# A two-layer encoder trunk: the norms' transposed copies on two engines, and block-sum steps later in some pairs of weight columns

## The chip, the cores and the metric

The kernel runs on one core of a Trainium2 chip. The metric is the device time of one execution in microseconds (us). A core has a matrix engine (TensorE, PE in the profile), a vector engine (VectorE, DVE), an activation engine (ScalarE, ACT), a general one (GpSimd, POOL) and a queue engine that issues loads here (SyncE, SP). They run side by side and wait for one another through semaphores; each runs its own instructions in program order. TensorE adds its products up in PSUM, in banks of 128 partitions by 512 floats; the other operands lie in SBUF.

## The reference

256 tokens of width 2048 pass through two layers. The first mixes tokens by attention, the second by a gated recurrence; each is followed by a gated feed-forward block (FFN) with 5632 hidden features. All is float32.

```python
def swiglu(h, w_gate, w_up, w_down):
    return (jax.nn.silu(h @ w_gate) * (h @ w_up)) @ w_down

for i in range(DEPTH):
    h = rms_norm(x, norm_mix[i])
    mix = attention_mixer(h, ...) if i % 2 == 0 else recurrent_mixer(h, ...)
    x = x + mix
    x = x + swiglu(rms_norm(x, norm_ffn[i]), ffn_w_gate[i], ffn_w_up[i], ffn_w_down[i])
```

`rms_norm` divides each token's row by the root of its mean square and scales each feature.

## The kernel before, in words

**Products.** Each float32 number is split into a high part and the rest (`hi` and `lo`, for weights; two halves of one tile for the other operand), and a product is three matmuls: hi times hi, hi times lo, lo times hi. Weights come in halves of 512 KB: SyncE's queue loads one into `raw`, ScalarE casts it to `hi` (L120), VectorE subtracts to get `lo` (L121). There are five buffers of each of the three, so a load starts when VectorE has read the raw half of five loads earlier, and a cast when TensorE is done with the half of five loads earlier.

**Pairs.** The FFN takes two output column blocks of 512 at a time (`project_pair`): gate and up together, or two columns of the down product. A pair keeps four PSUM banks (`acc`; two blocks by two groups of 128 tokens). It goes through its inner dimension in steps of two tiles of 128 features, two weight halves to a step. A gate/up pair has 8 steps over the 16 norm tiles `xg`. The hidden features come in three parts of 12, 16 and 16 tiles: a down pair of the first part has 6 steps, the others 8. A plain step is 24 matmuls. A block-sum step (steps 2 and 5 of 8, 1 and 3 of 6; `SEVEN`) is the seven-product form of a 2 by 2 block product, 21 matmuls: `seven_forms` adds weight blocks on VectorE (L245 to L248, into `wx`, which has one buffer), ScalarE casts the three sums (`wxh`, L252), VectorE subtracts (`wxl`, L253). Three of its products go to four extra banks `pm`, and after the pair's last block-sum step `merge` combines those on ScalarE and VectorE (L311 to L315) while TensorE goes on with the steps that are left.

**Ends of pairs.** After its last step a pair's banks are added on VectorE: to the merged blocks in a gate/up unit (L755, L758, each block followed by the nonlinearity), to the residual `x_tok` in a down product (L498; the merged blocks are added to it at L489). The next pair starts in the same four banks, one after the other, 6 matmuls each, so it wants the bank adds in that order.

**Turning.** Tokens lie on partitions in `x_tok`; the operands of the products need features there. `turned` does it for 512 features: two 32x32-blockwise transposes on VectorE into `tb`, then 16 copies of 32 partitions by 256 on ScalarE (L445) that put the blocks in place in `tf`. `tb` and `tf` have one buffer each. It serves two callers. `Norm.add` turns each of the four columns of `x_tok` as it is finished, and scales it into four `xg` tiles (hi on ScalarE L396, lo on VectorE L397): 12 calls. The FFN unit turns its 512 hidden features and casts them into four `act` tiles (L764, L765): 22 calls. In the unit the four hidden tiles of part 0 that come last are tiles 8 to 11, which steps 4 and 5 of a six-step pair multiply. Where a norm or a unit has both tiles of a block-sum step, `x_forms` makes that step's sums of the other operand (`nf`, `hf`).

**Order.** TensorE's order is the order of the program text. `ffn_order` lists the weight halves in the order in which pairs take them, which is the order of SyncE's loads. ScalarE's and VectorE's order is set by a scheduler, which places instructions by its own estimate of when their inputs are there.

Of the kernel before, what the change touches and what calls it, by code (L numbers as in the profile page):

```python
# [21 lines left out]
KT = D // P  # L22
# [4 lines left out]
DFF = 5632  # L27
PARTS = [12, 16, 16]
SEVEN = {6: (1, 3), 8: (2, 5)}
HALF = 8  # L30
WIDE = 512
NCOL = D // WIDE
FOUR = WIDE // P
# [37 lines left out]
def trunk(ctx, tc, w, out):  # L71
    nc = tc.nc
    act, dve, pool, pe, sync = nc.scalar, nc.vector, nc.gpsimd, nc.tensor, nc.sync
# [13 lines left out]
    def nm(s):  # L87
        uid[0] += 1
        return f"{s}_{uid[0]}"
# [17 lines left out]
    def load_half(src, n, pieces=1, then=None, before=None):  # L107
        raw = wp.tile([P, HALF, P], F32, tag="raw", name=nm("raw"), bufs=5)
        hi = wp.tile([P, HALF, P], F32R, tag="hi", name=nm("hi"), bufs=5)
        lo = wp.tile([P, HALF, P], F32R, tag="lo", name=nm("lo"), bufs=5)  # L110
        newest["load"] = sync.dma_start(out=raw[:, :n, :], in_=src[:, :n, :])
        newest["raw"] = raw
        if then:
            then()
        if before:
            before(raw)
        for i in range(pieces):
            sl = slice(i * n // pieces, (i + 1) * n // pieces)
            newest["tiles"] = hi, lo
            newest["cast"] = act.copy(hi[:, sl, :], raw[:, sl, :])  # L120
            dve.tensor_tensor(lo[:, sl, :], raw[:, sl, :], hi[:, sl, :].bitcast(F32), ALU.subtract)  # L121
        return [(hi[:, i, :], lo[:, i, :]) for i in range(n)]


    def halves(src, kt):
        return [(src[:, a : min(a + HALF, kt), :], min(HALF, kt - a)) for a in range(0, kt, HALF)]

    def wide(name):
        src = w[name]
        return [(src[c, i], HALF) for c in range(src.shape[0]) for i in range(src.shape[1])]  # L130

    def ffn_order(l):
        units = [wide(f"w_gate{l}"), wide(f"w_up{l}")]
        seq, i = [], 0
        for p, n in enumerate(PARTS):
            for _ in range(n // FOUR):
                seq += sum(zip(*(u[i : i + KT // 2] for u in units)), ())
                i += KT // 2
            down = wide(f"w_down{l}_{p}")
            for c in range(0, len(down), n):  # L140
                seq += sum(zip(down[c : c + n // 2], down[c + n // 2 : c + n]), ())
        return seq

    order = [(w["w_k"][i], HALF) for i in range(len(KEY_TILES))]
    order += sum((halves(w["w_qv"][h % 20], KT) for h in range(NQ, NQ + 20)), [])
    order += wide("w_o") + ffn_order(0)
    for b in range(-1, NBLK):
        xin = range(2 * b + 2, 2 * b + 4) if b + 1 < NBLK else []
        yin = range(KT + 2 * b, KT + 2 * b + 2) if b >= 0 else []
        both = [halves(w["w_in"][c], KT) for c in (*xin, *yin)]  # L150
# [35 lines left out]
    def step():  # L186
        clock[0] += 1
        due = [i for i, (t, _) in enumerate(waiting) if t <= clock[0]]
        if due:
            waiting.pop(due[0])[1]()  # L190
# [5 lines left out]
    def new_acc():  # L196
        return ps_a.tile([P, 2 * S], F32, tag="acc", name=nm("acc"))
# [37 lines left out]
    def flat(t):  # L235
        return t.rearrange("p (k c) f -> p k (c f)", k=2)
# [29 lines left out]
        dve.tensor_tensor(t[:, 1], y[:, 4:, :], t[:, 0].bitcast(F32), ALU.subtract)  # L266
        return [(t[:, 0, i, :], t[:, 1, i, :]) for i in range(4)]

    def project_pair(xs, forms, middle):
        banks = [[new_acc() for _ in range(2)] for _ in range(2)]  # L270
        begun = set()

        def product(acc, x, wt, last=False):
            for i, (a, b) in enumerate(((x[0], wt[0]), (x[0], wt[1]), (x[1], wt[0]))):
                pe.matmul(acc, a, b, start=id(acc) not in begun, stop=last and i == 2)  # L275
                begun.add(id(acc))
            step()
            step()

        def tokens(k, a):  # L280
            return [xs[k][:, o + a * P : o + (a + 1) * P] for o in (0, S)]

        end = len(xs) // 2 - 1
        for n in range(end + 1):
            if n in forms:
                s1, s2, s3, s4 = forms[n]
                b11, b21, t3, b22, t1, t2, t4 = seven_forms()
                if n == min(forms):
                    p1, q6, q5, q7 = (ps_m.tile([P, WIDE], F32, tag="pm", name=nm("pm")) for _ in range(4))
                last = n == max(forms)  # L290
                product(p1, tokens(2 * n, 0), b11, last)
                product(banks[0][0], tokens(2 * n + 1, 0), b21)
                product(banks[1][0], s4, b22)
                product(q7, s3, t3, last)
                product(q5, s1, t1, last)
                product(q6, s2, t2, last)
                product(banks[0][1], tokens(2 * n + 1, 1), t4)
                if last:
                    middle(p1, q5, q6, q7)
            else:  # L300
                for j in range(2):
                    half()
                    hi, lo = (flat(t) for t in newest["tiles"])
                    for a in range(2):
                        for k in range(2):
                            product(banks[j][a], tokens(2 * n + k, a), (hi[:, k, :], lo[:, k, :]), n == end and k == 1)
        return banks

    def merge(p1, q5, q6, q7):
        g, u = (fp[0].tile([P, 2, WIDE], F32, tag=t, name=nm(t), bufs=1) for t in ("fg", "fu"))  # L310
        act.copy(g[:, 0, :], p1)  # L311
        dve.tensor_tensor(g[:, 1, :], q6, g[:, 0, :], ALU.subtract)
        dve.tensor_tensor(u[:, 0, :], q5, g[:, 1, :], ALU.add)
        dve.tensor_tensor(g[:, 1, :], q7, g[:, 1, :], ALU.subtract)
        dve.tensor_tensor(u[:, 1, :], u[:, 0, :], q7, ALU.subtract)  # L315
        return g, u
# [66 lines left out]
    class Norm:  # L383
# [18 lines left out]
        def add(self, c):  # L402
            for a in range(2):
                act.activation(tmp("nj", (P, WIDE), bufs=1), x_tok[:, a, c, :], AF.Square, accum_out=self.sums[:, a, c : c + 1])
            for f in turned(x_tok[:, :, c, :]):
                self.operand(f, True)
            for n in SEVEN[KT // 2] if self.seven else ():
                if FOUR * c <= 2 * n < FOUR * c + FOUR:
# [24 lines left out]

    def turned(src):
        b = fp[0].tile([P, 2, FOUR, P], F32, tag="tb", name=nm("tb"))
        f = fp[0].tile([P, 8, FOUR, 32], F32, tag="tf", name=nm("tf"))
        for a in range(2):
            dve.transpose(b[:, a, :, :], src[:, a, :])  # L440
        for q in range(4):
            for i in range(4):
                o, y = f[32 * i : 32 * i + 32, q::4, :, :], b[32 * q : 32 * q + 32, :, i, :]
                y = y.rearrange("p a (k t) -> p a k t", k=FOUR)
                act.copy(o, y)  # L445
        return [f[:, :, k, :] for k in range(FOUR)]

    fp = []
# [65 lines left out]
    def table_act(*a, **k):  # L514
        table_op(act.activation(*a, **k))

    def ln_exp_tables():
        table_op(act.preload_act_table_set("natural_log_exp_and_others"))
# [191 lines left out]
    def act_tile():  # L710
        return xp.tile([P, 2 * S], F32R, tag="act", name=nm("act"), bufs=18)
# [35 lines left out]


    def ffn(norm, nxt):
        def unit(hid, forms, seven):  # L750
            got = []
            banks = project_pair(norm.xs, norm.forms, lambda *banks: got.extend(merge(*banks)))
            g, u = got
            for a, acc in enumerate(banks[0]):
                dve.tensor_tensor(g[:, a, :], acc, g[:, a, :], ALU.add)  # L755
                table_act(g[:, a, :], g[:, a, :], AF.Silu, scale=norm.rt[:, a : a + 1])
            for a, acc in enumerate(banks[1]):
                dve.tensor_tensor(u[:, a, :], acc, u[:, a, :], ALU.add)  # L758
                dve.scalar_tensor_tensor(u[:, a, :], u[:, a, :], norm.rt[:, a : a + 1], g[:, a, :], ALU.mult, ALU.mult)
            first = len(hid)  # L760
            for f in turned(u):
                h = act_tile()
                hi, lo = (h[:, o : o + S].rearrange("p (q t) -> p q t", t=32) for o in (0, S))
                act.copy(hi, f)  # L764
                dve.tensor_tensor(lo, f, hi.bitcast(F32), ALU.subtract)  # L765
                hid.append(h)
            for i, n in enumerate(seven):
                if first <= 2 * n < len(hid):
                    forms[n] = x_forms(hid[2 * n], hid[2 * n + 1], f"hf{i}")

        for p, n in enumerate(PARTS):
            hid, forms = [], {}
            for _ in range(n // FOUR):
                unit(hid, forms, SEVEN[n // 2])
            last = p == len(PARTS) - 1
            if last and nxt is not None:
                ln_exp_tables()
            down(hid, forms, nxt if last else None, last and nxt is None)
# [106 lines left out]
    units = [(d, j) for j in range(2) for d in range(2)]  # L885
# [114 lines left out]
```

## Time and profile before

| what | us |
|---|---|
| three runs: lowest, median, highest | 2032.6, 2037.86, 2040.56 |
| the profiled execution | 2037.47 |
| its span | 2035.7 |
| TensorE busy in it | 1996.2 (98%) |
| VectorE busy | 1692.5 (83%) |
| ScalarE busy | 1369.3 (67%) |

The span is what the profiler saw between the first and the last instruction. Each row of a timeline is a start, a duration, the engine, the line, the operation, what it writes and reads (tile names without numbers), and in brackets the idle time before it with what ended it. The profile shows also the TensorE clock that the throttle granted, 1.00 being full speed; over the profiled span it was 0.992.

### The profile page before, as it was taken

How to read it: one execution, taken by the hardware profiler on the slowest of the kernel's cores; microseconds unless marked ns; L12 is line 12 of the kernel's file. 1: busy time of each engine (PE TensorE's matmuls, PEld its weight loads, DVE VectorE, ACT ScalarE, POOL GpSimd, SP SyncE). 2: the span in 40 equal slices, each digit the busy share in tenths (PEclk: the TensorE clock that was granted, in tenths of full speed). 3: DMA queues.
4: the chain of work that ended last, by engine and by line, in shares of the span. 5: the costliest groups of instructions: out<-in, count | busy, mean ns of one | idle time of the engine just before them, and what ended most of it. 6: DMA issues, size and time to landing. Idle time of an engine off the chain costs nothing.

```text
span 2035.7 us, 27908 instructions
## 1 busy us (share of the span) xinstructions
PE 1996.2 (98%) x9920; PEld 1689.5 (83%) x9920; DVE 1692.5 (83%) x2351; ACT 1369.3 (67%) x2166; POOL 168.7 (8%) x213
## 2 busy tenths in 40 slices
PE   9999999999999999999799999999999999999999
PEld 8898878878888888887699998878788878888887
DVE  8998678987888888888679887688897888878887
ACT  7665876664667446677789988767745766457663
POOL 1563000000000000000133330000000000000000
PEclk9999999999999999999899999999999999999999
DMA  8444555556555665655456554656556556655564
GB/s 320 156 135 145 194 180 194 188 191 196 191 201 183 222 197 189 205 184 196 155 172 187 184 176 158 207 167 205 186 188 195 188 199 213 196 193 187 199 217 145
DMA packets 109003, 386.06 MB, mean 190 GB/s; under 512 B 12224, under 2 KB 12992, under 8 KB 108736
## 3 DMA queue, kind: packets, MB, share of 16 engines
q1 hardware_dynamic: 108720, 384.26, 57.1%
q8 instruction: 78, 1.28, 0.2%
q14 instruction: 61, 0.50, 0.1%
q10 hardware_dynamic: 144, 0.02, 0.0%
HBM read 382.13 MB, written 2.10 MB: 189 GB/s over the span
## 4 chain that ended last, share of the span: by engine, by line
PE 47%; issue 42%; DVE 7%; DMA 2%; ACT 2%; POOL 0%; SPq 0%; DVEq 0%; ACTq 0%; POOLq 0%
PE acc L275 23%; PE acc L228 4%; PE acc L206 4%; PE pm L275 3%; DVE lo L121 3%; PE acc L319 3%; PE acc L320 3%; PE acc L321 3%; PE pm L320 1%; PE pm L321 1%; PE pm L319 1%; DMA raw<-in_w_up_dram 1%; ACT tf L445 1%; ACT hi L120 1%; DMA raw<-in_w_down_dram 0%
## 5 line engine op out<-in xcount | busy, mean ns | idle before, releaser
L120 ACT CAST hi<-raw 128x1024 fp32r<-128x1024 f32 (+1 forms) x708 | 727.6, 1045 | 477.6 <-PE acc L275 372.1
L121 DVE TENSOR_TENSOR lo<-raw,hi 128x1024 fp32r<-128x1024 f32 (+1 forms) x708 | 852.4, 1223 | 135.3 <-ACT hi L120 133.9
L275 PE MATMUL acc<-hi,xg 128*128 128x512 f32 x2200 | 697.7, 390 | 3.0 <-DVE fg L755 2.9
L275 PEld LDWEIGHTS acc<-hi,xg 128*128 128x128 f32 x2200 | 413.8, 188 | 95.5 <-issue 6.4
L275 PE MATMUL acc<-lo,xg 128*128 128x512 f32 x1100 | 428.6, 390 | 0.0
L275 PE MATMUL acc<-hi,act 128*128 128x512 f32 x1072 | 342.6, 391 | 0.9 <-DVE fg L755 0.7
L275 PEld LDWEIGHTS acc<-lo,xg 128*128 128x128 f32 x1100 | 207.0, 188 | 42.3
L275 PEld LDWEIGHTS acc<-hi,act 128*128 128x128 f32 x1072 | 201.9, 188 | 48.4 <-issue 3.0
L445 ACT COPY tf<-tb 32x256 f32<-32x256 f32 x544 | 219.5, 404 | 9.2 <-DVE xg L397 1.0
L275 PE MATMUL acc<-lo,act 128*128 128x512 f32 x536 | 209.2, 390 | 0.0
L228 PE MATMUL acc<-hi,act 128*128 128x512 f32 x512 | 159.9, 390 | 0.0
L319 PE MATMUL acc<-xg,hi 128*128 128x256 f32 x512 | 147.0, 287 | 11.7 <-ACT xg L396 11.7
L320 PE MATMUL acc<-xg,hi 128*128 128x256 f32 x512 | 146.6, 286 | 0.5 <-DVE xg L397 0.5
L245 DVE TENSOR_TENSOR wx<-raw,raw 128x512 f32<-128x512 f32 x68 | 47.0, 691 | 119.7 <-DMA raw<-in_w_up_dram 91.5
L321 PE MATMUL acc<-xg,lo 128*128 128x256 f32 x512 | 146.0, 285 | 0.0
L253 DVE TENSOR_TENSOR wxl<-wx,wxh 128x1536 fp32r<-128x1536 f32 x68 | 119.1, 1752 | 22.4 <-ACT wxh L252 22.1
L206 PE MATMUL acc<-xg,hi 128*128 128x512 f32 x384 | 125.7, 396 | 0.2 <-ACT hi L120 0.2
L252 ACT CAST wxh<-wx 128x1536 fp32r<-128x1536 f32 x68 | 100.3, 1476 | 34.5 <-DVE wx L248 34.5
L275 PEld LDWEIGHTS acc<-lo,act 128*128 128x128 f32 x536 | 100.9, 188 | 20.4
L228 PEld LDWEIGHTS acc<-hi,act 128*128 128x128 f32 x512 | 96.1, 188 | 19.6
L319 PEld LDWEIGHTS acc<-xg,hi 128*128 128x128 f32 x512 | 99.8, 195 | 12.1 <-ACT xg L396 12.1
L320 PEld LDWEIGHTS acc<-xg,hi 128*128 128x128 f32 x512 | 99.7, 195 | 1.1 <-DVE xg L397 1.0
(238 smaller groups left out, 2830.4 us busy)
## 6 DMA issues: line engine op xcount, KB each, us to landing
raw<-in_w_gate_dram SPq DMA_DIRECT2D x176, 512.0 KB, 4.4
raw<-in_w_up_dram SPq DMA_DIRECT2D x176, 512.0 KB, 4.3
raw<-in_w_down_dram SPq DMA_DIRECT2D x176, 512.0 KB, 4.3
raw<-in_w_in_dram SPq DMA_DIRECT2D x64, 512.0 KB, 4.5
raw<-in_w_qv_dram SPq DMA_DIRECT2D x40, 512.0 KB, 4.3
raw<-in_w_o_dram SPq DMA_DIRECT2D x32, 512.0 KB, 3.6
raw<-in_w_out_dram SPq DMA_DIRECT2D x32, 512.0 KB, 4.3
graw<-in_w_gates_dram SPq DMA_DIRECT2D x32, 256.0 KB, 3.5
```

The lines of the kernel that those rows point to most:

```text
L120: newest["cast"] = act.copy(hi[:, sl, :], raw[:, sl, :])
L121: dve.tensor_tensor(lo[:, sl, :], raw[:, sl, :], hi[:, sl, :].bitcast(F32), ALU.subtract)
L206: pe.matmul(o, w, x, start=(k == 0 and not part), stop=(k == total - 1 and not part))
L228: pe.matmul(accs[a], x, wt[:, k, :], start=(k0 + k == 0 and n == 0), stop=(end and k == 1 and n == 2))
L245: dve.tensor_tensor(x[:, 0, :], r2[:, 0, :], r1[:, 0, :], ALU.add)
L252: act.copy(xh, x)
L253: dve.tensor_tensor(xl, x, xh[:].bitcast(F32), ALU.subtract)
L275: pe.matmul(acc, a, b, start=id(acc) not in begun, stop=last and i == 2)
L319: pe.matmul(o, hi, x[:, :S], start=start, stop=False)
L320: pe.matmul(o, hi, x[:, S:], start=False, stop=False)
L321: pe.matmul(o, lo, x[:, :S], start=False, stop=stop)
L445: act.copy(o, y)
```

## The change

It has three parts. In `turned`, the odd two of every four copies go to VectorE when the norms call it: 96 of the 192 copies of the 12 calls. The units pass `False` and keep ScalarE for all 16. In the first gate/up pair of each layer the steps run in the order 0, 1, 3, 4, 2, 6, 5, 7, so that the block-sum steps 2 and 5 stand fifth and seventh. In each pair of six steps the order is 0, 2, 1, 4, 3, 5, so that block-sum steps 1 and 3 stand third and fifth; there are two such pairs in each layer. The loads follow (`ffn_order`), and the first and last block-sum step, and the last step, are taken from the new order. All other pairs keep theirs. The number of matmuls, loads and casts stays.

```diff
+USUAL_STEPS = {6: (0, 2, 1, 4, 3, 5), 8: (0, 1, 2, 3, 4, 5, 6, 7)}
+FIRST_STEPS = (0, 1, 3, 4, 2, 6, 5, 7)
...
+    def pair_steps(n, first=False):
+        return FIRST_STEPS if first else USUAL_STEPS[n]
+
     def ffn_order(l):
...
-                seq += sum(zip(*(u[i : i + KT // 2] for u in units)), ())
+                for k in pair_steps(KT // 2, i == 0):
+                    seq += [u[i + k] for u in units]
                 i += KT // 2
             down = wide(f"w_down{l}_{p}")
             for c in range(0, len(down), n):
-                seq += sum(zip(down[c : c + n // 2], down[c + n // 2 : c + n]), ())
+                for k in pair_steps(n // 2):
+                    seq += [down[c + k], down[c + n // 2 + k]]
...
-    def project_pair(xs, forms, middle):
+    def project_pair(xs, forms, middle, first=False):
...
-        end = len(xs) // 2 - 1
-        for n in range(end + 1):
+        steps = pair_steps(len(xs) // 2, first)
+        seven = [n for n in steps if n in forms]
+        for n in steps:
             if n in forms:
...
-                if n == min(forms):
+                if n == seven[0]:
...
-                last = n == max(forms)
+                last = n == seven[-1]
...
-                            product(banks[j][a], tokens(2 * n + k, a), (hi[:, k, :], lo[:, k, :]), n == end and k == 1)
+                            product(banks[j][a], tokens(2 * n + k, a), (hi[:, k, :], lo[:, k, :]), n == steps[-1] and k == 1)
...
-    def turned(src):
+    def turned(src, both=True):
...
-                act.copy(o, y)
+                if i % 2 and both:
+                    dve.tensor_copy(o, y)
+                else:
+                    act.copy(o, y)
...
-            for f in turned(u):
+            for f in turned(u, False):
...
-            for _ in range(n // FOUR):
-                unit(hid, forms, SEVEN[n // 2])
+            for i in range(n // FOUR):
+                unit(hid, forms, SEVEN[n // 2], p == i == 0)
```

Three places show what this does to the order of an engine's instructions. The numbers behind the names tell tiles apart; a line such as L498 of the kernel before is L509 in the changed one.

VectorE at the end of the first six-step pair of layer 0, before. `lo` are halves of the next pair's weights, `fg` and `fu` the merged blocks, `acc_4364`, `4366`, `4365` and `4367` the four banks, in the order in which the next pair wants them:

```order
L314 TENSOR_TENSOR fg_4528<-pm_4428,fg_4528 128x512
L315 TENSOR_TENSOR fu_4529<-fu_4529,pm_4428 128x512
L489 TENSOR_TENSOR x_tok<-x_tok,fu_4529 128x512
L246 TENSOR_TENSOR raw_4664<-raw_4664 128x512
L121 TENSOR_TENSOR lo_4657<-raw_4655,hi_4656 128x1024
L498 TENSOR_TENSOR x_tok<-x_tok,acc_4364 128x512
L489 TENSOR_TENSOR x_tok<-x_tok,fg_4528 128x512
L489 TENSOR_TENSOR x_tok<-x_tok,fu_4529 128x512
L247 TENSOR_TENSOR wx_4661<-raw_4664,raw_4655 128x512
L498 TENSOR_TENSOR x_tok<-x_tok,acc_4366 128x512
L121 TENSOR_TENSOR lo_4666<-raw_4664,hi_4665 128x1024
L498 TENSOR_TENSOR x_tok<-x_tok,acc_4365 128x512
```

The same place in the changed kernel:

```order
L252 TENSOR_TENSOR wx_4697<-raw_4700,raw_4691 128x512
L509 TENSOR_TENSOR x_tok<-x_tok,acc_4364 128x512
L321 TENSOR_TENSOR fu_4565<-pm_4463,fg_4564 128x512
L253 TENSOR_TENSOR raw_4700<-raw_4700 128x512
L322 TENSOR_TENSOR fg_4564<-pm_4464,fg_4564 128x512
L323 TENSOR_TENSOR fu_4565<-fu_4565,pm_4464 128x512
L500 TENSOR_TENSOR x_tok<-x_tok,fu_4565 128x512
L123 TENSOR_TENSOR lo_4675<-raw_4673,hi_4674 128x1024
L254 TENSOR_TENSOR wx_4697<-raw_4700,raw_4691 128x512
L500 TENSOR_TENSOR x_tok<-x_tok,fg_4564 128x512
L500 TENSOR_TENSOR x_tok<-x_tok,fu_4565 128x512
L509 TENSOR_TENSOR x_tok<-x_tok,acc_4366 128x512
```

The merge now stands between the first and the second bank add, and a sum of the next block-sum step's weights (`wx_4697`, which reads the load `raw_4700`) ahead of both. After the last row shown come `lo_4693`, `wx_4697`, and then the adds of `acc_4365` and `acc_4367`.

ScalarE in the first six-step pair of layer 0, before. `tf_4333` holds the hidden features of the unit just ended, `act_4352` and `act_4355` are hidden tiles 8 and 9, `wxh` the block-sum step's weight sums:

```order
L120 CAST hi_4496<-raw_4495 128x1024
L120 CAST hi_4540<-raw_4539 128x1024
L445 COPY tf_4333<-tb_4332 32x2x128 x16
L120 CAST hi_4558<-raw_4557 128x1024
L252 CAST wxh_4493<-wx_4492 128x1536
L120 CAST hi_4576<-raw_4575 128x1024
L764 CAST act_4352<-tf_4333 128x256
L764 CAST act_4355<-tf_4333 128x256
```

And in the changed kernel:

```order
L122 CAST hi_4505<-raw_4504 128x1024
L456 COPY tf_4333<-tb_4332 32x2x128 x16
L122 CAST hi_4523<-raw_4522 128x1024
L122 CAST hi_4532<-raw_4531 128x1024
L122 CAST hi_4576<-raw_4575 128x1024
L775 CAST act_4352<-tf_4333 128x256
L775 CAST act_4355<-tf_4333 128x256
L775 CAST act_4358<-tf_4333 128x256
L775 CAST act_4361<-tf_4333 128x256
L259 CAST wxh_4529<-wx_4528 128x1536
```

The cast of the sums has gone behind the casts of the hidden tiles. On TensorE the plain step 4, which multiplies tiles 8 and 9, stands ahead of the second block-sum step instead of behind it.

ScalarE at the last norm column of layer 0's FFN, before. `nj` is the norm's square sum, `tf_3237` the turned column, `xg` the norm tiles, `wxh_3362` the sums of the first pair's first block-sum step:

```order
L404 ACTIVATE nj_3234,nsq_2358<-x_tok 128x512
L120 CAST hi_3365<-raw_3364 128x1024
L120 CAST hi_3402<-raw_3401 128x1024
L445 COPY tf_3237<-tb_3236 32x2x128 x16
L515 ACTIVATE rsq_s_3272<-nrt_3268 128x2
L252 CAST wxh_3362<-wx_3361 128x1536
L120 CAST hi_3420<-raw_3419 128x1024
```

And in the changed kernel:

```order
L412 ACTIVATE nj_3234,nsq_2358<-x_tok 128x512
L456 COPY tf_3237<-tb_3236 32x2x128 x8
L122 CAST hi_3374<-raw_3373 128x1024
L404 ACTIVATE xg_3256<-tf_3237,pk 128x256
L404 ACTIVATE xg_3259<-tf_3237,pk 128x256
L404 ACTIVATE xg_3262<-tf_3237,pk 128x256
L404 ACTIVATE xg_3265<-tf_3237,pk 128x256
L122 CAST hi_3392<-raw_3391 128x1024
L526 ACTIVATE rsq_s_3272<-nrt_3268 128x2
L122 CAST hi_3410<-raw_3409 128x1024
L526 ACTIVATE nr_3271<-rsq_s_3272 128x2
L122 CAST hi_3428<-raw_3427 128x1024
```

Eight copies are left there, the norm tiles come directly behind them, and the cast of the sums (`wxh_3434`) has moved two rows past the end of what is shown.

More of the change, by code (lines that the diff above doesn't have):

```diff
@@ L749, in ffn, with unit @@
     def ffn(norm, nxt):
-        def unit(hid, forms, seven):
+        def unit(hid, forms, seven, first):
             got = []
-            banks = project_pair(norm.xs, norm.forms, lambda *banks: got.extend(merge(*banks)))
+            banks = project_pair(norm.xs, norm.forms, lambda *banks: got.extend(merge(*banks)), first)
             g, u = got
```

## Prediction

> **What bounds the kernel now.** I read the page first, for the engines' shares, then the waits of TensorE, and then the timeline around each wait that the change touches.
>
> ```profile
> span 2035.7 us, 27908 instructions
> PE 1996.2 (98%) x9920; PEld 1689.5 (83%) x9920; DVE 1692.5 (83%) x2351; ACT 1369.3 (67%) x2166; POOL 168.7 (8%) x213
> ```
>
> TensorE is busy for 98% of the span, so the time moves only by what it waits for, and by what its clock does after a wait. About 39 us separate its busy time from the span. Which engine it waited for (total, times, longest):
>
> ```profile
> PE acc L319 <- ACT xg L396: 11.7, 2, 8.4
> PE pm L275 <- ACT wxh L252: 6.3, 4, 2.0
> PE pm L275 <- DVE wxl L253: 6.2, 5, 1.3
> PE acc L275 <- DVE fg L755: 3.6, 6, 1.4
> ```
>
> The first row is the start of the recurrence; rows two and three are block-sum steps that want their three cast weight sums; the last is the start of a pair that wants its accumulator banks back. One such block-sum step, in the first gate/up pair:
>
> ```profile
> 274.38 6.65 ACT L445 COPY tf<-tb 32x256 f32<-32x256 f32 x16
> 281.16 1.46 ACT L252 CAST wxh<-wx 128x1536 fp32r<-128x1536 f32 x1
> ...
> 282.65 1.76 DVE L253 TENSOR_TENSOR wxl<-wx,wxh 128x1536 fp32r<-128x1536 f32 x1 [5.32 <-ACT wxh L252]
> ...
> 281.08 0.39 PE L275 MATMUL pm<-hi,nf 128*128 128x512 f32 x1
> 282.67 0.50 PE L275 MATMUL pm<-wxh,nf 128*128 128x512 f32 x1 [1.20 <-ACT wxh L252]
> 284.46 0.50 PE L275 MATMUL pm<-wxl,nf 128*128 128x512 f32 x1 [1.29 <-DVE wxl L253]
> ...
> 288.91 0.39 PE L275 MATMUL acc<-lo,xg 128*128 128x512 f32 x1
> ```
>
> The cast of the sums stands on ScalarE behind the norm's 16 copies; VectorE's wxl follows the cast; TensorE waits for both. How fast the matmuls then run (stretch, TensorE busy with its count, the other engines, granted clock, DMA):
>
> ```profile
> 283.00:288.20 5.20, 3.91 (x12) 2.93 (x12) 5.20 (x7) 5.10 (x9) 0.00 (x0) 0.73 0.27 83
> 290.00:300.00 10.00, 10.00 (x45) 8.28 (x45) 7.84 (x10) 5.39 (x5) 0.00 (x0) 1.00 0.72 241
> ```
>
> 45 matmuls in 10 us are 0.222 from start to start; I use 0.227. The wxh wait therefore cost 282.67 − 281.08 − 0.23 = 1.36, the wxl wait 284.46 − 282.67 − 0.23 = 1.56, and the 12 matmuls from 284.46 to 288.91 took 4.45 where 2.72 is full speed: 1.73 more, at a granted clock below 1. Together 4.65.
>
> **First pairs.** Steps 2 and 5 become the fifth and seventh, so the first wxh is wanted two plain steps later. A plain step is 24 matmuls, 5.45; a block-sum step 21, 4.77. Wanted at 281.3 + 10.9 = 292.2, against a wxl that even in the old order ends at 284.4. All 4.65 goes, in each layer: **−9.3**. What is late next is the end of this pair. Only one plain step is left behind the last block-sum step, and in it VectorE does the merge, a weight sum that waits for its load, and the bank adds. That place has this shape nowhere before; the nearest row is the longest bank wait:
>
> ```profile
> 1649.53 0.47 PE L275 MATMUL acc<-hi,xg 128*128 128x512 f32 x1 [1.36 <-DVE fg L755]
> ```
>
> I take 0.9, between 0.3 and 1.5, twice: **+1.8**.
>
> **First six-step pair.** The fourth step before is a block-sum step:
>
> ```profile
> 411.18 6.63 ACT L445 COPY tf<-tb 32x256 f32<-32x256 f32 x16
> 418.79 1.47 ACT L252 CAST wxh<-wx 128x1536 fp32r<-128x1536 f32 x1
> 421.11 1.32 ACT L764 CAST act<-tf 128x256 fp32r<-128x256 f32 x4
> ...
> 418.00 0.39 PE L275 MATMUL pm<-hi,hf 128*128 128x512 f32 x1
> 420.31 0.50 PE L275 MATMUL pm<-wxh,hf 128*128 128x512 f32 x1 [1.91 <-ACT wxh L252]
> 422.10 0.79 PE L275 MATMUL pm<-wxl,hf 128*128 128x512 f32 x1 [1.29 <-DVE wxl L253]
> ...
> 425.51 0.40 PE L275 MATMUL acc<-hi,act 128*128 128x512 f32 x1
> ```
>
> By the same reckoning it loses 2.08 + 1.56 + 1.6 (8 intervals from 422.10 to 425.51) = 5.2. In the new order the fourth step is plain step 4, which multiplies hidden tiles 8 and 9. These come from the unit just ended: transposes, 16 copies on ScalarE (the units keep them there), casts of the tiles, low halves. The fourth step starts twelve matmuls ahead of 418.2, at 415.5; with 0.4 for a bank wait that I add at the pair's start, 415.9. The copies have one weight cast less ahead of them (1.05): 410.1 to 416.75. Then the order has three weight casts (0.96 apart, 419.7 with what they hand over), then tile 8's cast and VectorE's low half: about 420.95. TensorE waits 5.05 (4 to 6), and runs at the reduced clock after it, 1.7 by the row above. New 5.05 + 0.4 + 1.7 = 7.15, old 5.2: +1.95, in two layers **+3.9** (−1.6 with 4 and no clock loss, +5.8 with 6). The second six-step pair of a layer has all its tiles early; it pays only at its end.
>
> **Ends of the six-step pairs.** Four pairs now end block-sum, plain, where two plain steps stood last. On VectorE the merge, its four adds into x_tok, the weight halves of the next pair and the four bank adds fall into 5.45. Before, the second such pair of layer 0 ends like this:
>
> ```profile
> 465.13 0.68 DVE L498 TENSOR_TENSOR x_tok<-x_tok,acc 128x512 f32<-128x512 f32 x1
> ...
> 466.93 1.22 DVE L121 TENSOR_TENSOR lo<-raw,hi 128x1024 fp32r<-128x1024 f32 x1
> 468.07 0.68 DVE L498 TENSOR_TENSOR x_tok<-x_tok,acc 128x512 f32<-128x512 f32 x1
> ...
> 469.27 0.68 DVE L498 TENSOR_TENSOR x_tok<-x_tok,acc 128x512 f32<-128x512 f32 x1
> ...
> 468.14 0.39 PE L275 MATMUL acc<-hi,xg 128*128 128x512 f32 x1
> ```
>
> A 128x512 operation takes 0.60 of VectorE's time, a low half 1.14. Adds are done as TensorE wants each bank: at 0, 1.36, 2.72 and 4.1 after the pair's end. In the new order (shown for the first pair) a weight sum wx stands ahead of the first bank add. It waits for a load into the slot that the low half of five loads earlier frees. How long that takes, before:
>
> ```profile
> 347.46 1.22 DVE L121 TENSOR_TENSOR lo<-raw,hi 128x1024 fp32r<-128x1024 f32 x1
> ...
> 353.24 0.69 DVE L245 TENSOR_TENSOR wx<-raw,raw 128x512 f32<-128x512 f32 x1 [1.51 <-DMA raw<-in_w_up_dram]
> ```
>
> 4.56 from the low half's end to the sum. I count from the pair's end. TensorE frees the slot's cast buffers at −10.2 (4.77 + 5.45); the cast takes 1.05 and the low half 1.22: −7.8. The sum starts at −3.25 by 4.56; with the transfers less crowded at a pair's end I take −3.8. From it seven operations of 0.60 (sum, first bank add, three of the merge, a raw sum, an x_tok add) reach +0.4, a low half 1.54, three more 3.34, the second bank add ends at 4.0. TensorE wants that bank at 1.36 and waits 2.7. Behind it stand a low half, a sum and the third bank add: 6.4, wanted at 2.72 + 2.7 = 5.4, 1.0 more. So 3.75 with rounding (2.9 to 4.2 as the load comes), four times, less the 0.6 already lost before: +14.4.
>
> Whether the clock drops after such a wait, two rows bound:
>
> ```profile
> 1002.34:1006.00 3.66, 3.66 (x17) 3.43 (x18) 1.66 (x4) 1.52 (x4) 0.20 (x4) 0.56 0.12 30
> ...
> 1647.00:1652.00 5.00, 3.64 (x17) 2.70 (x16) 5.00 (x8) 2.58 (x3) 0.00 (x0) 1.00 0.34 105
> ```
>
> 0.56 after a wait of 3.3, 1.00 around one of 1.36. 3.75 in two pieces lies between them; I take half of 1.7: 0.8 each, +3.2. **+17.6** (11.0 to 23.0).
>
> [...]
>
> **Recurrence start.** The last two norm columns are turned there while TensorE has nothing else:
>
> ```profile
> 985.61 6.60 ACT L445 COPY tf<-tb 32x256 f32<-32x256 f32 x16
> 995.14 6.61 ACT L445 COPY tf<-tb 32x256 f32<-32x256 f32 x16 [1.01 <-DVE xg L397]
> ...
> 992.89 0.58 PE L319 MATMUL acc<-xg,hi 128*128 128x256 f32 x1 [8.39 <-ACT xg L396]
> 1002.34 0.58 PE L319 MATMUL acc<-xg,hi 128*128 128x256 f32 x1 [3.26 <-ACT xg L396]
> ```
>
> The durations of the kinds that matter, over the whole run:
>
> ```profile
> L121 DVE TENSOR_TENSOR lo<-raw,hi 128x1024 fp32r<-128x1024 f32 x702 | 849.7, 1230 | 134.9 <-ACT hi L120 133.6
> L445 ACT COPY tf<-tb 32x256 f32<-32x256 f32 x544 | 219.5, 404 | 9.2 <-DVE xg L397 1.0 <-DVE tb L440 0.8
> L356 DVE CAST qs<-hq 128x256 fp32r<-128x256 f32 x16 | 4.6, 288 | 0.4 <-POOL hq L588 0.4
> ```
>
> ScalarE keeps eight copies, 3.3, and VectorE does eight beside it. No 32x256 copy on VectorE is in the trace; by the 128x256 cast 8 x 0.288 = 2.3, by ScalarE's own 3.3, so ScalarE ends last by either. Each set is 3.3 shorter: 992.89 becomes 989.6, and the second start 995.7 instead of 1002.34. The work between them, 992.89 to 1002.34 − 3.26, is 6.2 at the reduced clock, so the second wait is all but gone: −6.6, and part of the reduced clock behind it (17 matmuls in 3.66): 1.1. **−7.7** (−5.0 if the copies queue behind two low halves, −8.3 if all the clock loss goes). [...]
>
> SyncE's queue issues the same loads, two halves of 512 KB for each step, in the new order of the steps, and ScalarE's and VectorE's casts of them move along; number, size and room of the buffers stay, so I put 0 on it beyond the wait for a slot above. Everywhere else the 96 copies moved (ScalarE −38.8, VectorE +27.7 in all) lie beside TensorE's work: the first pairs have 7.8 of slack by the reckoning above, and outside them VectorE is busy 83%. The fifth wxl wait is in a pair that stays.
>
> Sum: −9.3 + 1.8 + 3.9 + 17.6 − 7.7 = +6.3. The profiled execution took 2037.47 us, 0.4 under the median of 2037.86, so the sum gives **2043.7**; its ends together, −8.9 and +18.5, give 2028.6 and 2056.
>
> **Rivals.** Slower: the clock falls after every one of the four six-step ends and the load lands at the late value, 4 x (4.2 + 1.7) − 0.6 = 23.0, sum +11.7, **2049.2**. For it speaks the 0.73 behind two short waits, against it the 1.00 at 1647. It decides from 21.5 at these four places on. Faster: VectorE keeps up, because the load lands sooner or the lateness is absorbed, and no bank is late: −9.3 + 3.9 − 7.7, **2024.4**. For it speaks that before only 3.6 us go to banks; against it the count above. Hidden tiles in time: no 5.05 and no 1.7, 13.5 less, **2030.2**; this needs the copies to end five us sooner, for which no row speaks. The split brings nothing at the recurrence, since VectorE's copies stand behind casts of loads: +7.7, **2051.4**; VectorE has no low halves left there in the old trace, where ScalarE's copies are the wait.
>
> **How the numbers follow.** Forecast 0.45 (its own range 2035 to 2051), slower rival 0.22, faster 0.15, hidden tiles in time 0.08, no gain from the split 0.10. A measurement tells 0.5%, 10.2 us, from no change. Faster takes most of 0.15 and some of 0.08: 0.17. Slower takes two thirds of 0.22, most of 0.10 and the upper end of the forecast: 0.31. Same 0.52. The range goes from the faster rival to the upper bound of the sum: 2024 to 2057.
>
> **What would show it.** The waits on wxh and wxl lose four times each; no stretch near 283 has a clock under 1. Around 416 TensorE waits on tiles' casts (act). Bank waits on the second and third x_tok adds appear at the four ends, 2.7 and 1.0. The two waits on xg sum to about 5 instead of 11.7. I am wrong if the bank waits stay under 1, if they are longer than 4.2, or if step 4 starts on time.

## The result, and the profile after

The changed kernel takes 2040.42 us in the median against 2038.68 for the kernel before, 20 runs each; the ratio is 1.0012, with an interval of 1.0002 to 1.0021. One of the 20 runs before took 4580.54 us and is not in the ratio. The change is about 2 us slower, inside the half per cent that the prediction counts as no change. The profiled execution took 2042.2 us, 4.7 more than the one of before. It is among the three slowest of the 20, so the traces show more of a difference than the medians do.

The page of the changed kernel: VectorE has taken on 29 us of work, ScalarE has lost 33, and TensorE's share is what it was.

```profile
span 2040.4 us, 27933 instructions
...
PE 1999.7 (98%) x9920; PEld 1691.3 (83%) x9920; DVE 1721.6 (84%) x2447; ACT 1336.3 (65%) x2070; POOL 166.6 (8%) x213
```

The waits of TensorE (total, times, longest) read quite differently:

```profile
PE acc L282 <- DVE x_tok L509: 11.1, 7, 2.4
PE acc L282 <- ACT act L775: 7.5, 2, 3.8
PE acc L282 <- DVE fg L766: 4.5, 10, 0.9
PE acc L327 <- ACT xg L404: 3.4, 1, 3.4
...
PE pm L282 <- DVE wxl L260: 1.4, 1, 1.4
```

The cast of the sums (wxh) is gone from the list, and wxl has left the first pairs; the wait on xg fell from 11.7 to 3.4. In their place stand waits on bank adds into `x_tok`, which were not in the list, and on hidden tiles (`act`). Where they are, in TensorE's timeline:

```profile
312.07 0.50 PE L282 MATMUL acc<-hi,xg 128*128 128x512 f32 x1 [0.46 <-DVE fg L766]
...
415.49 0.80 PE L282 MATMUL acc<-hi,act 128*128 128x512 f32 x1 [3.76 <-ACT act L775]
...
417.16 1.22 PE L282 MATMUL acc<-hi,act 128*128 128x512 f32 x2 [0.45 <-DVE act L776]
...
438.59 0.50 PE L282 MATMUL acc<-hi,act 128*128 128x512 f32 x1 [2.32 <-DVE x_tok L509]
...
474.30 0.50 PE L282 MATMUL acc<-hi,xg 128*128 128x512 f32 x1 [2.40 <-DVE x_tok L509]
476.73 0.47 PE L282 MATMUL acc<-hi,xg 128*128 128x512 f32 x1 [0.78 <-DVE x_tok L509]
...
996.21 0.58 PE L327 MATMUL acc<-xg,hi 128*128 128x256 f32 x1 [3.45 <-ACT xg L404]
```

From here on I count a place by its excess: at each matmul the time to the start of the next, less 0.227 us for 512 columns or 0.120 for 256 (the median spacing of such matmuls in the trace of before), summed over the place. It holds the wait and the slow clock behind it. By place, in us:

| place | before | after |
|---|---|---|
| first gate/up pairs: waits on the sums | 4.63 + 4.64 | 0 |
| their ends: bank waits | 0 | 0.73 + 0.73 |
| first six-step pairs, with the bank wait at their start | 5.20 + 7.06 | 8.24 + 8.69 |
| ends of the four six-step pairs | 0.37 + 0 + 0.37 + 0 | 4.28 + 3.69 + 6.11 + 4.70 |
| recurrence's start | 17.01 | 7.70 |

The sum of these rows rises from 39.3 to 44.9, by 5.6; the spans differ by 4.7. About 18.6 us were won in two rows and 24.2 lost in the other three.

### The profile page after: what moved, and what is told of

Its sections match the earlier page's. It is cut to its first block, busy times and chain, and to the rows that moved or that the text cites. A ratio compares the mean times of both kernels' runs of the same rounds, so it can differ in the third digit from the quotient of the medians.

```text
span 2040.4 us, 27933 instructions
## 1 busy us (share of the span) xinstructions
PE 1999.7 (98%) x9920; PEld 1691.3 (83%) x9920; DVE 1721.6 (84%) x2447; ACT 1336.3 (65%) x2070; POOL 166.6 (8%) x213
## 4 chain that ended last, share of the span: by engine, by line
PE 69%; DVE 17%; DMA 6%; issue 5%; ACT 3%; SPq 0%; POOL 0%; DVEq 0%; ACTq 0%
PE acc L282 38%; PE acc L235 8%; DVE lo L123 7%; PE pm L282 5%; PE acc L213 5%; DMA raw<-in_w_up_dram 4%; PE acc L328 3%; PE acc L327 3%; PE acc L329 3%; ACT tf L456 1%; DMA raw<-in_w_down_dram 1%; ACT hi L122 1%; PE pm L328 1%; PE pm L329 1%; PE pm L327 1%
## 5 line engine op out<-in xcount | busy, mean ns | idle before, releaser
L282 PE MATMUL acc<-hi,act 128*128 128x512 f32 x1072 | 349.7, 399 | 14.9 <-ACT act L775 7.5
L456 ACT COPY tf<-tb 32x256 f32<-32x256 f32 x448 | 181.2, 404 | 8.4 <-DVE xg L405 1.2
L235 PE MATMUL acc<-hi,act 128*128 128x512 f32 x512 | 159.8, 390 | 0.0
```

The lines of the kernel that those rows point to most:

```text
L235: pe.matmul(accs[a], x, wt[:, k, :], start=(k0 + k == 0 and n == 0), stop=(end and k == 1 and n == 2))
```

## Experiments

**One part at a time.** In the first, only the norms' copies are split; the steps stand as before.

```diff
-USUAL_STEPS = {6: (0, 2, 1, 4, 3, 5), 8: (0, 1, 2, 3, 4, 5, 6, 7)}
-FIRST_STEPS = (0, 1, 3, 4, 2, 6, 5, 7)
+USUAL_STEPS = {6: (0, 1, 2, 3, 4, 5), 8: (0, 1, 2, 3, 4, 5, 6, 7)}
+FIRST_STEPS = (0, 1, 2, 3, 4, 5, 6, 7)
```

> Only the split of the norms' copies; both step orders as before. Theory (each part acts at its own place, and the parts add): the recurrence's start loses about 9 us of waiting and slow clock, as between the two traces (17.0 us over full speed from 980 to 1012 before, 7.8 after), and nothing else moves: -9 us, ratio 0.9956. Rival (VectorE's extra copies make it late elsewhere, and it is they that bring the bank waits at the ends of the six-step pairs): the gain at the recurrence is eaten, ratio 1.000 or above, with waits on x_tok adds here too.

Measured: 2023.29 us, ratio 0.9928 (0.9913 to 0.9944), some 15 us less where 9 were expected. The recurrence's start costs 7.68, as in the changed kernel (7.70), so that term is the split's. The surplus comes from the first pairs. ScalarE there, with the split alone:

```profile
273.56 3.31 ACT L456 COPY tf<-tb 32x256 f32<-32x256 f32 x8 [0.47 <-DVE tb L448]
276.90 2.00 ACT L122 CAST hi<-raw 128x1024 fp32r<-128x1024 f32 x2
278.81 1.71 ACT L404 ACTIVATE xg<-tf,pk 128x256 fp32r<-128x256 f32 x4
```

The copies take 3.31 instead of 6.65, and TensorE has no wait at all between 275 and 292. So the split removes the waits on the sums at these pairs without any new order of steps; at the ends of these pairs 0.5 and 1.3 of excess appear. The split and the first pairs' order solve the same wait twice, and their gains do not simply add.

**The first pairs' order alone:** copies all on ScalarE (`both=False` for the norms too), six-step pairs as before.

> Only the first gate/up pair's new order in each layer; copies and six-step pairs as before. Theory: the waits on wxh and wxl at 281 and 1332 and the slow clock behind them go (4.66 and 4.69), a bank wait of about 0.7 comes at the end of each of these pairs: -7.9 us, ratio 0.9961. Rival (without the split ScalarE's 16 copies still make the sums late, or the pair's end is the worse for it): half of that or less, ratio 0.998 to 1.000.

Measured: 2024.44 us, ratio 0.9941 (0.9924 to 0.9959): −12 where −7.9 was expected. The waits at 281 and 1332 are gone, and 0.7 and 1.7 of excess with bank waits stand at the ends. A place that I had not counted gains too, the first six-step pair. Its old order now waits 0.55 for the cast of the sums instead of 1.91, and the place costs 3.97 and 2.40 in the two layers, for 5.20 and 6.63 before.

```profile
413.89 0.49 PE L282 MATMUL pm<-wxh,hf 128*128 128x512 f32 x1 [0.55 <-ACT wxh L259]
...
415.68 0.50 PE L282 MATMUL pm<-wxl,hf 128*128 128x512 f32 x1 [1.30 <-DVE wxl L260]
```

**The six-step order alone.**

> Only the new order of the six-step pairs. Theory: about 4.4 us for the wait for hidden tiles in place of the wait for the sums, and 18 for the four ends: +22 us, ratio 1.011. Rival (it needs the split's load on VectorE to make the ends late): +5 us or less, ratio below 1.003.

Measured: 2056.7 us, ratio 1.0094 (1.0079 to 1.0109), about +19 where +22 was expected. The order makes its waits without the split:

```profile
PE acc L282 <- DVE x_tok L509: 12.7, 9, 2.3
PE acc L327 <- ACT xg L404: 11.9, 2, 8.4
PE acc L282 <- ACT act L775: 7.3, 2, 3.7
```

They are the size of those in the changed kernel (11.1 and 7.5). The rival, that VectorE's extra copies are needed for it, falls.

**All but the six-step order.**

> The changed kernel with the old order of the six-step pairs: the split and the first pairs only. Theory: -9 - 7.9 = -17 us, 2021, ratio 0.9917; the wait for the sums in the first six-step pair (5.45 and 6.7 with slow clock) is back. Rival (the six-step order is not what costs): within 5 us of the changed kernel, ratio 0.999 or above.

Measured: 2016.64 us, ratio 0.9899 (0.9885 to 0.9914): −20.6. The six-step order thus costs some 23 us in the changed kernel (1.0012 against 0.9899), and this is the fastest kernel of the study that computes the whole result. The split alone gave 15 and the first pairs' order alone 12, the two together 20.6. The waits in its first six-step pairs cost 3.98 and 2.39, for 5.20 and 6.63 before. The expectation said that the old ones would be back; they are smaller, as in the run with the first pairs' order alone. There the order still gains beside the split, which leaves 5.23 and 5.11 at this place.

**Two plain steps at the end.** The six-step pairs go 0, 2, 1, 3, 4, 5, the rest as in the changed kernel.

```diff
-USUAL_STEPS = {6: (0, 2, 1, 4, 3, 5), 8: (0, 1, 2, 3, 4, 5, 6, 7)}
+USUAL_STEPS = {6: (0, 2, 1, 3, 4, 5), 8: (0, 1, 2, 3, 4, 5, 6, 7)}
```

> The changed kernel with the six-step pairs in the order 0, 2, 1, 3, 4, 5: block-sum steps third and fourth, two plain steps at the end, hidden tiles 8 and 9 wanted at the fifth step. Theory (the one plain step at the end is what leaves VectorE no room): the waits on x_tok adds at the four ends, 18.8 us with the slow clock, go to under 1 each, and so does the wait on act. A wait on the sums in the first six-step pair takes its place, since their cast now stands behind the casts of the hidden tiles on ScalarE: 5 us and slow clock, twice. Together 12 to 18 us under the changed kernel, ratio to before 0.992 to 0.995. Rival (the ends are late because the next pair's load lands late, whatever the order): the x_tok waits stay near 2.4, and the ratio is 1.000 or above.

Measured: 2029.26 us, ratio 0.9967 (0.9954 to 0.998), 9 us under the changed kernel, where 12 to 18 were expected.

```profile
PE acc L282 <- DVE fg L766: 7.0, 10, 1.4
PE pm L282 <- ACT wxh L259: 5.5, 2, 2.8
PE pm L282 <- DVE wxl L260: 5.2, 5, 1.4
```

No wait on `x_tok` is left, and none on `act`. The four ends cost nothing (0.7 within each second pair is a wait on wxl), so the position of the last block-sum step decides the ends. The new wait on the sums came as expected, dearer: 8.7 in each layer, of which 0.8 and 0.8 are waits for the casts and low halves of the weights themselves. The expectation had put 5 and some slow clock there, so this took back a part of the gain.

**Hidden tiles.** The changed kernel, with half of the copies of each layer's third unit on VectorE.

```diff
-            for f in turned(u, False):
+            for f in turned(u, both):
...
-                unit(hid, forms, SEVEN[n // 2], p == i == 0)
+                unit(hid, forms, SEVEN[n // 2], p == i == 0, p == 0 and i == 2)
```

> The changed kernel; the third unit of part 0 in each layer, whose tiles are 8 to 11, also has half of its 16 copies on VectorE. Theory (ScalarE's 16 copies make the hidden tiles late): tiles 3.3 us sooner, the wait on act falls from 3.8 to about 0.5 in both layers and the slow clock behind it goes, 6 us each: -12 against the changed kernel, ratio to before 0.995; the ends keep their waits. Rival (they are late by the casts of weights between copies and tiles, which wait for TensorE): the wait stays above 3, ratio 1.000 to 1.001.

Measured: 2032.82 us, ratio 0.9984 (0.9974 to 0.9993), 5.7 us under the changed kernel where 12 were expected; its profiled span is 9.4 shorter. The wait on ScalarE's casts of the tiles is gone (the place costs 0.70 and 0.69 where it cost 7.49 and 8.08):

```profile
404.97 3.32 ACT L456 COPY tf<-tb 32x256 f32<-32x256 f32 x8
408.31 1.06 ACT L122 CAST hi<-raw 128x1024 fp32r<-128x1024 f32 x1
409.27 1.32 ACT L775 CAST act<-tf 128x256 fp32r<-128x256 f32 x4
```

Eight copies less are 3.3 us. But one weight cast now stands ahead of the tiles' casts where three stood (412.19 in the changed kernel, shown further down), 1.9 us more, so this run does not tell the copies' share from the casts'. The rival that the casts wait there for TensorE falls by the changed kernel's own rows: between copies and tiles ScalarE has no pause beyond 0.02 us (the copies end at 412.17, the three casts run from 412.19 to 415.13, and the tiles' casts start at 415.04). Part of what was won is given back at the end of the same pair, where the two layers' excess rises from 4.28 + 6.11 to 6.37 + 7.08:

```profile
433.44 0.56 PE L282 MATMUL acc<-hi,act 128*128 128x512 f32 x1 [4.51 <-DVE x_tok L509]
```

2.32 has become 4.51. TensorE starts the last matmul ahead of this wait 7.3 us earlier than in the changed kernel (428.54 for 435.88), VectorE ends the second bank add only 5.2 earlier (433.38 for 438.54): VectorE has 0.14 of idle time from 420 to 434 in this run, and a second low half stands between the merge and the second bank add. So the wait on the tiles had covered a part of VectorE's lateness.

**VectorE's volume or the load.** The changed kernel without the adds of the merged blocks in six-step pairs; that part of the down product is left out.

```diff
-                for j, t in enumerate((g, u)):
+                for j, t in () if len(xs) == 12 else enumerate((g, u)):
```

> The changed kernel without the four adds of the merged blocks into x_tok in each six-step pair; that part of the down product is left out. Three of the four stand ahead of the second bank add. Theory (VectorE's volume between the merge and the bank adds makes the banks late): the second bank add comes 1.8 us sooner or more, the waits of 2.2 to 2.4 on it fall under 0.6, the four ends cost 2 to 5 us in all where they cost 18.8, and the run is 12 to 16 us under the changed kernel. Rival (the weight sum's wait for its load): the adds only idle instead, waits stay at 2 or more, and less than 4 us are gained.

Measured once: 2027.63 us, 9 us under the kernel before on the same chip where the changed kernel is 2 over it, so about 11 less; the span is 14.6 shorter, and 12 to 16 were expected. All four ends run without a wait. The stretch that held the 2.32 wait (TensorE busy and count, clock, DMA):

```profile
430.00:440.00 10.00, 10.00 (x44) 1.00 0.48 159
```

and VectorE in it:

```profile
430.85 0.69 DVE L252 TENSOR_TENSOR wx<-raw,raw 128x512 f32<-128x512 f32 x1 [0.46 <-DMA raw<-in_w_down_dram]
...
434.45 0.68 DVE L509 TENSOR_TENSOR x_tok<-x_tok,acc 128x512 f32<-128x512 f32 x1
...
435.65 1.22 DVE L123 TENSOR_TENSOR lo<-raw,hi 128x1024 fp32r<-128x1024 f32 x1
```

The sum still waits for its load, 0.46 now, and the second bank add is done in time. Three adds are gone from ahead of it, and in this kernel's order the low half, too, stands behind it. So what VectorE does ahead of that add decides, not the load. In the changed kernel's own trace the same chain is:

```profile
465.48 0.69 DVE L320 TENSOR_TENSOR fg<-pm,fg 128x512 f32<-128x512 f32 x1
466.42 0.69 DVE L252 TENSOR_TENSOR wx<-raw,raw 128x512 f32<-128x512 f32 x1 [0.25 <-DMA raw<-in_w_up_dram]
467.02 0.68 DVE L509 TENSOR_TENSOR x_tok<-x_tok,acc 128x512 f32<-128x512 f32 x1
...
470.62 1.22 DVE L123 TENSOR_TENSOR lo<-raw,hi 128x1024 fp32r<-128x1024 f32 x1
...
473.56 0.68 DVE L509 TENSOR_TENSOR x_tok<-x_tok,acc 128x512 f32<-128x512 f32 x1
...
475.90 1.28 DVE L509 TENSOR_TENSOR x_tok<-x_tok,acc 128x512 f32<-128x512 f32 x2
```

From `fg` at 465.48 to the end of the second bank add at 474.24 are 8.8 us; 0.25 of them is the wait for the load, the rest is twelve operations of 0.60 and a low half of 1.14, 8.3 in all, almost without a pause. At the third of the four ends the sum waits for no load at all (1481.16), and TensorE waits 2.17 there all the same.

**The wait on the sums in the old six-step order.** Step orders of before, norms' copies split, and the third unit's too (the edit of the hidden tiles, on the first experiment's kernel).

> The step orders of before, the norms' copies split, and the third unit's copies of part 0 split too. Against the run with the norms' split alone (ratio 0.9928, waits on the sums in the first six-step pair of 5.2 and 5.1 with slow clock). Theory (what ScalarE has ahead of the cast of the sums sets that wait): 3.3 us fewer of copies stand ahead, but the order puts the casts of the four hidden tiles and one more weight cast there, 2.3, so the cast of the sums comes 1.0 sooner and the wait on it falls from 2.0 to about 1.0: ratio 0.991 to 0.993. Rival (it goes by the number of copies alone): the wait is gone, 5 us in each layer, ratio 0.988.

Measured: 2023.62 us, ratio 0.9943 (0.9922 to 0.9965), no different from the split of the norms alone (0.9928). The wait itself changed engines:

```profile
415.12 0.49 PE L282 MATMUL pm<-wxh,hf 128*128 128x512 f32 x1 [0.83 <-ACT wxh L259]
418.12 0.80 PE L282 MATMUL pm<-wxl,hf 128*128 128x512 f32 x1 [2.51 <-DVE wxl L260]
```

ScalarE's cast came sooner, as the theory says: 0.83 of waiting. VectorE now has eight copies (2.38) ahead of the subtraction, and in its order the low halves of the four tiles (1.43) as well. It subtracts no sooner for TensorE than with the split alone: the two waits are 3.34 together, where they were 1.94 and 1.29. The place costs 6.48 and 5.19, with the split alone 5.23 and 5.11. Neither expectation had VectorE next in line.

**A milder order for the first pairs.** Split of the norms' copies, old six-step order, first pairs in the order 0, 1, 3, 2, 4, 5, 6, 7.

> Split of the norms' copies, old order of the six-step pairs, and the first gate/up pairs in the order 0, 1, 3, 2, 4, 5, 6, 7: the first block-sum step is fourth, the second sixth, and two plain steps stand at the end. Against the run with split and the fifth/seventh order (ratio 0.9899, bank waits of 0.7 at the end of these pairs). Theory (one plain step at the end of a pair is too little for VectorE): the bank waits at 311 and 1352 fall under 0.2, and no wait on the sums comes back at 281 and 1332, since the split alone already removed it: 1.4 us less at these places, ratio 0.988 to 0.992. Rival (the first pairs' end is late by the norm's own late work on VectorE): the 0.7 stays.

Measured: 2021.66 us, ratio 0.9918 (0.9901 to 0.9936). The bank waits at 311 and 1352 are gone. The two stretches around them, with fifth and seventh first:

```profile
308.00:316.00 8.00, 7.59 (x34) 1.00 0.31 82
1349.00:1357.00 8.00, 7.51 (x33) 1.00 0.33 90
```

and with fourth and sixth:

```profile
308.00:316.00 8.00, 8.00 (x36) 1.00 0.50 169
1349.00:1357.00 8.00, 8.00 (x37) 1.00 0.63 197
```

The theory on the ends holds in gate/up pairs too. The time is no better, since the wait in the first six-step pairs is back at 5.12 and 6.13, for 3.98 and 2.39 with fifth and seventh. The traces of layer 0 show where the difference begins. With fifth and seventh (and old six-step order) VectorE makes the raw sum (L253) at 401.80, and ScalarE's copies start at 404.87. With the split alone the raw sum comes at 405.15, behind one of the transposes, and the copies start at 407.91: 3.0 later, while TensorE comes to the wait only 1.6 later. Why the scheduler gives VectorE another order there after another order of an earlier pair stays open, and no run holds the one and changes the other.

## Why the prediction was right

It forecast 2043.7 and "same" from a sum of +6.3; the profiled execution came out at 2042.2 and the median at 2040.42. By the medians the change is about +2, a third of the sum; the terms below are those of the profiled execution. Two ends of the sum were added up wrongly: its printed bounds give −7.6 and +17.5, not −8.9 and +18.5. The terms, as excess by place:

| term | predicted | measured |
|---|---|---|
| first pairs, waits on the sums | −9.3 | −9.3 |
| their ends | +1.8 | +1.5 |
| first six-step pairs | +3.9 | +4.7 |
| ends of the six-step pairs | +17.6 | +18.0 |
| recurrence's start | −7.7 | −9.3 |
| sum | +6.3 | +5.6 |

*First pairs.* The size is right, and the order of the steps is enough for it, as the run with that order alone shows. But it was counted as the only cause, and the split removes the same 9.3 by itself. That the copies at the norms "lie beside TensorE's work" holds for these pairs only with the new order: with the order of before they are on the path, and halving them frees it. In the changed kernel this cannot be seen, because both act.

*First six-step pair.* The wait on hidden tiles was to be 5.05 and is 3.76 and, for the low half, 0.45 (0.93 in the second layer). ScalarE's sequence is the one counted, eight rows of its timeline in three:

```profile
412.19 2.94 ACT L122 CAST hi<-raw 128x1024 fp32r<-128x1024 f32 x3
415.04 1.32 ACT L775 CAST act<-tf 128x256 fp32r<-128x256 f32 x4
416.26 1.47 ACT L259 CAST wxh<-wx 128x1536 fp32r<-128x1536 f32 x1
```

The slow clock behind it (0.50 from 415.5 to 420.0 and from 1468.4 to 1472.9) made good the difference: 2.8 and 3.1 without a wait, where 1.7 was taken.

*Ends.* The waits of 2.32, 2.40, 2.17 and 2.42 on the second bank answer to 2.7, those on a third bank (0.78, 0.60, 0.44, none at the first) to 1.0. The sum `wx` starts 3.94 to 4.20 before the pair's end, where −3.8 was taken. The load sets that start at three of the four ends, as counted, but it is not why VectorE is late, and this reason in the step is wrong. It delays VectorE by 0.17, 0.25, 0 and 0.27, because VectorE's work ahead of the sum, low halves and the first operation of the merge, ends only a little earlier. The rival "VectorE keeps up, because the load lands sooner" could not have come true that way: an earlier load would have given 0.27 at most.

*Slow clock at the ends.* 0.8 each was taken between 0 and 1.7; what stands there outside the waits (the excess of each end less that at its waits) is 1.8, 0.2, 2.8 and 1.3, 6.1 in all for the 3.2 of the sum. The upper bound of 1.7 was passed at two ends, and the shorter waits made up for it. That 18.0 stands beside 17.6 is therefore in part luck of this execution: with the six-step order alone, where the waits are nearly the same, the four ends cost 14.3, which is 13.5 more than before. The slower rival asked for the clock to drop behind every end; it did behind three (0.57, 0.67 and 0.64, with 1.00 behind the second), and the sum of its place stayed at 18.0, under the 21.5 from which it decides.

*Recurrence's start.* The work between the two sets now fills the second wait, as reckoned. The first wait is 3.45 and 0.66 instead of 5.1, so the gain went 1.0 past the far end given for this term (−8.3). The count held only the copies' duration. Before, they start at 985.61, 1.1 after TensorE stops (992.89 − 8.39 = 984.5); now VectorE's start at 990.59, 2.2 before it stops (996.21 − 3.45 = 992.76). Of these 3.3 a norm's square and a weight cast, which the new order puts ahead of `xg`, take back about half (994.09 to 995.66). The copies on VectorE take 0.285, by 0.288 from the row that was used:

```profile
990.59 2.38 DVE L454 COPY tf<-tb 32x256 f32<-32x256 f32 x8
```

2.38 for eight, 0.299 from start to start. That is more than the 0.285 that a copy lasts, so in this trace they do not overlap, while the 128x512 sums above, 0.68 long, start every 0.60.

## What to carry to other kernels

Measure the parts of a change apart before counting them as a sum: here two parts removed the same wait, and a third lost more than both gained at other places. A late step at the end of a stage has to be weighed by what the engine that hands back the buffers must do in the time left; count its operations from the first to the one that is waited for. A wait that goes can uncover the next engine's lateness: it moved from ScalarE to VectorE in one run (waits of 0.83 and 2.51 where 1.94 and 1.29 stood), and from tiles to banks in another (4.51 where 2.32 stood).

## What was not expected of the hardware

Nearly equal waits left very different clocks. The 4 us behind the four bank waits of 2.32, 2.40, 2.17 and 2.42 us (TensorE busy and count, granted clock, DMA share, GB/s):

```profile
438.60:442.60 4.00, 4.00 (x10) 0.57 0.36 118
474.30:478.30 4.00, 3.22 (x13) 1.00 0.40 126
1489.00:1493.00 4.00, 3.36 (x10) 0.67 0.41 96
1526.80:1530.80 4.00, 3.56 (x10) 0.64 0.36 119
```

The run with the six-step order alone waits 2.21, 2.27, 2.30 and 2.32 at these places, each time 0.76 or 0.77 more at the next bank, and keeps full clock behind all four:

```profile
440.00:444.00 4.00, 3.22 (x13) 1.00 0.37 112
474.90:478.90 4.00, 3.24 (x13) 1.00 0.33 102
1501.60:1505.60 4.00, 3.11 (x12) 1.00 0.39 102
1536.60:1540.60 4.00, 3.16 (x13) 1.00 0.38 123
```

So the clock after a short wait isn't given by its length: 2.40 left it at 1.00 and 2.17 brought it to 0.67. What else sets it is not shown: no run here moved one of these waits and held the rest fixed.
